# Gate build of a PEER layer: float32 products for every other u block, gate blocks stored by expert

## The chip, the cores and the metric

The kernel runs on one core of a Trainium2 chip. The metric is the device time of one execution in microseconds. Its engines are TensorE (PE, with its weight loads as PEld), VectorE (DVE), ScalarE (ACT) and GpSimd (POOL), and the queue of SyncE (SP) issues most of the DMAs.

## The reference, cut to what matters

The model is two transformer blocks on 512 tokens of width 1024. The change lies in the expert layer (PEER) of the first block, which the reference writes as a gather:

```
q = (xb @ w_query).reshape(128, 8, 2, 128)
s = einsum('chpd,hpnd->chpn', q, sub_keys)
top_s, top_i = lax.top_k(s, 16)             # two lists of 16 of 128 keys
cand_s = top_s[:, :, 0, :, None] + top_s[:, :, 1, None, :]
cand_i = top_i[:, :, 0, :, None] * 128 + top_i[:, :, 1, None, :]
best_s, pos = lax.top_k(cand_s, 16);  idx = take_along_axis(cand_i, pos)
g = softmax(best_s)
act = gelu(einsum('cd,chkd->chk', xb, expert_u[idx]))
out = einsum('chk,chkd->cd', g * act, expert_v[idx])
```

There are 16384 experts, and each token uses 8 x 16 of them.

## The kernel before, in words

The first 128 tokens are done by gathering: GpSimd fetches the rows of u and v that they need, and VectorE multiplies them (L1078, L1084, L1092). The other 384 tokens (TD) are done densely: all 16384 experts are cut into 128 blocks of 128, and for block b the kernel computes acts(b) = gelu(u(b) h) (384 tokens in the free dimension), multiplies by the gates of that block, and adds the product with v(b) into six PSUM banks named vac. A gate is zero where a token does not use an expert.

**Split products.** A float32 weight tile wr that the Stream class has loaded is split by ACT into a high part wh (L110) and by another engine into a low part wl (L111); each product is then three fp32r matmuls (L198 to L200, in lin and mm3). The hidden state hA is split in the same way; hD is its part for the 384 tokens. The stream holds four wr tiles (WR = 4); add names the tiles in the order in which they are loaded, and get splits three tiles ahead. For the u blocks of the gate build the low part is made on GpSimd (lo=G).

**Gate build** (L1027 to L1035). The gates are built from one-hot matrices, eight tokens (GS) at a time, in 48 groups. For each group VectorE makes oj and oi (L995) and og, the second one times the gate (L1002); TensorE multiplies them token by token into a 128 x 128 tile pG (L1018, L1019), and ACT copies it into a stage tile st (L1020). One st holds all 128 blocks of 128 experts for 64 tokens (ST); there are two. When an st is full, SP writes it to DRAM in four DMAs, one for each quarter of the blocks (gates, L1024). Between the groups, u blocks 12 to 33 are multiplied (u_side: pA), so that 34 blocks of acts (AHEAD) are ready before the main loop.

**Main loop** (L1118 on). Step b multiplies u block b + 34, loads the gates of block b + 3 (gate_load: gt, L1049), makes the weighed activations of block b + 1 (weigh, L1053 to L1056), and multiplies block b with v. Beside it run the gathers for the first 128 tokens, whose row tiles lie where st lay.

The order on each engine is made when the kernel is built, by a scheduler that may move instructions within the dependences; each engine then runs its list in order. SP issues its DMAs in list order, waiting where a buffer is still in use.

Of the kernel before, what the change touches and what calls it, by code (L numbers as in the profile page):

```python
# [20 lines left out]
P = 128  # L21
S = 512
D = 1024
# [11 lines left out]
AHEAD = 34  # L35
ST = 64
ROWS, LAG = 7, 5
# [7 lines left out]
FNV = (1, 3)  # L45
GSCALE = 4096.0
WR, WH, SD = 4, 5, 3
RB = 1
# [29 lines left out]
class Stream:  # L78


    def __init__(self, nc, pool):
        self.nc, self.pool, self.items, self.out, self.raw = nc, pool, [], {}, {}
        self.d = self.s = 0

    def add(self, key, src, dest=None, lo=None):
        self.items.append((key, src, dest, lo))
# [9 lines left out]
    def _split(self):  # L96
        i = self.s
        if self.d <= i:
            self._load()
        key, src, dest, lo_eng = self.items[i]  # L100
        n = src.shape[1]
        raw = self.raw.pop(i)
        if dest is None:
            hi = self.pool.tile([P, 512], FR, name=f"wh{i}", tag="wh", bufs=WH)[:, :n]
            lo = self.pool.tile([P, 512], FR, name=f"wl{i}", tag="wl", bufs=WH)[:, :n]
        else:
            hi, lo = dest()
        if len(hi.shape) == 3:
            raw = raw.rearrange("p (k n) -> p k n", n=P)
        self.nc.scalar.activation(hi, raw, AF.Copy)  # L110
        (lo_eng or self.nc.vector).tensor_tensor(lo, raw, hi.bitcast(FT), op=OP.subtract)  # L111
        self.out[key] = (hi, lo)
        self.s += 1
# [43 lines left out]
def body(ctx, tc, a):  # L157
# [253 lines left out]
    n_early = len(u_at) + U_TAIL  # L411

    def add_u(b, **kw):
        for c in range(2):
            ws.add(("u", b, c), a["uT"][b][:, c * 512:(c + 1) * 512], **kw)

    for m in range(16):
        for c in range(2):
            ws.add(("qy", m, c), a["w_query"][m][:, c * 512:(c + 1) * 512], lo=G)
        if m in u_at:  # L420
            add_u(u_at[m], lo=G)
    for b in range(len(u_at), AHEAD):
        add_u(b, lo=G)
    late = {}

# [352 lines left out]
    late["h0"] = h0  # L778
    hn = pk.tile([P, D], FT, name="hn")
    gw0 = pk.tile([P, P], FT, name="gw0")  # L780
    idx = pk.tile([P, P], I32, name="idx")
# [196 lines left out]

    gd = [nc.dram_tensor(f"gates{q}", (TD // ST, P, P // 4, ST), FT, kind="Internal").ap() for q in range(4)]
    ps = ps.then(pA=2, pG=4, rest=2)  # L980
    s1 = ExitStack()
    pg = pool(s1, "pgb", OGB)

    def u_side(b):
        w = [ws.get(("u", b, c)) for c in range(2)]
        pa_ = ps.tile([P, TD], FT, name=f"pA{b}", tag="pA")
        lin(pa_, w, KD, slice(0, TD), lambda k: hD[:, 0, k], lambda k: hD[:, 1, k])
        last["gelu"] = A.activation(acts[:, b % AA], pa_, AF.Gelu).ins  # L988
# [21 lines left out]
    def gate_sum(g, oj, og):  # L1010
# [10 lines left out]
        if t0 + GS == ST:  # L1021
            st = stage.pop(n)
            for q in range(4):
                nc.sync.dma_start(gd[q][n], st[:, q * (P // 4):(q + 1) * (P // 4)])  # L1024

    hot = []
    NG = TD // GS  # L1027
    for i in range(NG):
        hot.append(gate_hot(i))
        if len(hot) > 1:  # L1030
            gate_sum(*hot.pop(0))
        for b in range(n_early + i * (AHEAD - n_early) // NG, n_early + (i + 1) * (AHEAD - n_early) // NG):
            u_side(b)
    while hot:
        gate_sum(*hot.pop(0))  # L1035
    s1.close()

# [4 lines left out]
    act = pac.tile([P, P], FT, name="act")  # L1042
    acc = pac.tile([P, D], FT, name="acc")
    late["tile"] = lambda n, nm: pac.tile([P, n], FR, name=f"late{nm}")
    gates = {}

    def gate_load(b):
        gates[b] = pg.tile([P, TD], FT, name=f"gt{b}", tag="gt", bufs=4)
        nc.sync.dma_start(gates[b].rearrange("p (n t) -> p n t", t=ST), gd[b // 32][:, :, b % 32].rearrange("n j t -> j n t"))  # L1049

# [60 lines left out]
    vac = [ps.tile([P, 512], FT, name=f"vac{i}", tag=f"vac{i}") for i in range(6)]  # L1111
    for b in range(3):
        gate_load(b)
# [461 lines left out]
```

## Time and profile before

| | us |
|---|---|
| median of 3 runs | 2120.83 (2117.81 to 2125.31) |
| profiled execution | 2124.07 |
| its span | 2122.3 |
| TensorE busy | 2033.1 (96%) |
| VectorE busy | 1540.5 (73%) |
| ScalarE busy | 884.8 (42%) |
| GpSimd busy | 645.1 (30%) |
| DMA packets | 267426, of them 119297 under 512 bytes |

The gate build runs from about 462 to 629 us of the span, the main loop from there to about 1540 us. Shares over the whole span hide stages: the same engine can be the bound in one and wait in the next. A row of a stretch gives for each engine its busy time and count, then the granted TensorE clock as a part of full speed, the mean busy share of the 16 DMA engines, and GB/s. "Idle before" in a row is the time for which the engine waited, and the name behind it is what ended the wait.

### The profile page before, as it was taken

How to read it: one execution, taken by the hardware profiler on the slowest of the kernel's cores; microseconds unless marked ns; L12 is line 12 of the kernel's file. 1: busy time of each engine (PE TensorE's matmuls, PEld its weight loads, DVE VectorE, ACT ScalarE, POOL GpSimd, SP SyncE). 2: the span in 40 equal slices, each digit the busy share in tenths (PEclk: the TensorE clock that was granted, in tenths of full speed). 3: DMA queues.
4: the chain of work that ended last, by engine and by line, in shares of the span. 5: the costliest groups of instructions: out<-in, count | busy, mean ns of one | idle time of the engine just before them, and what ended most of it. 6: DMA issues, size and time to landing. Idle time of an engine off the chain costs nothing.

```text
span 2122.3 us, 31628 instructions
## 1 busy us (share of the span) xinstructions
PE 2033.1 (96%) x10907; PEld 1738.9 (82%) x10907; DVE 1540.5 (73%) x3202; ACT 884.8 (42%) x1748; POOL 645.1 (30%) x545
## 2 busy tenths in 40 slices
PE   7999989889998999999999999999989999999999
PEld 5765778788887899999999999988868578888887
DVE  7879879999986877777777777768887854333322
ACT  4477443255553443333433333344443744333321
POOL 2235325765523433333333333323123400000000
PEclk9989999999999999999999999999989999999999
DMA  7514522225669999999998999989943122222332
GB/s 267 179 45 161 182 84 76 90 90 197 251 227 315 353 312 309 301 296 307 295 307 294 312 294 303 301 269 316 300 134 100 41 65 75 96 98 97 97 115 74
DMA packets 267426, 425.90 MB, mean 201 GB/s; under 512 B 119297, under 2 KB 123265, under 8 KB 264194
## 3 DMA queue, kind: packets, MB, share of 16 engines
q1 hardware_dynamic: 224866, 284.15, 40.9%
q0 software_dynamic: 36864, 134.23, 18.5%
q10 hardware_dynamic: 5536, 5.51, 0.9%
q8 instruction: 85, 1.39, 0.3%
q14 instruction: 75, 0.61, 0.1%
HBM read 391.83 MB, written 29.36 MB: 198 GB/s over the span
## 4 chain that ended last, share of the span: by engine, by line
PE 72%; DVE 19%; DMA 3%; issue 2%; ACT 2%; POOL 1%; SPq 0%; ACTq 0%; DVEq 0%; POOLq 0%
PE vac L199 7%; PE vac L200 7%; PE vac L198 7%; PE pA L198 6%; PE pA L199 6%; PE pA L200 6%; DVE og L1002 3%; DVE oi L995 2%; PE pd L199 2%; PE pd L198 2%; PE pd L200 2%; PE upp L200 2%; PE upp L199 2%; PE upp L198 2%; PE gatep L199 2%
## 5 line engine op out<-in xcount | busy, mean ns | idle before, releaser
L110 ACT ACTIVATE wh<-wr 128x512 fp32r<-128x512 f32 x716 | 448.4, 629 | 883.0 <-PE vac L200 220.2
L111 DVE TENSOR_TENSOR wl<-wr,wh 128x512 fp32r<-128x512 f32 x616 | 427.1, 697 | 404.7 <-ACT wh L110 403.4
L198 PE MATMUL pA<-hA,wh 128*128 128x384 f32 x928 | 315.7, 340 | 8.8 <-ACT acts L988 4.7
L200 PE MATMUL pA<-hA,wl 128*128 128x384 f32 x928 | 313.2, 338 | 0.0
L199 PE MATMUL pA<-hA,wh 128*128 128x384 f32 x928 | 312.5, 337 | 0.0
L200 PE MATMUL vac<-wh,wwl 128*128 128x512 f32 x759 | 297.7, 392 | 0.0
L199 PE MATMUL vac<-wl,wwh 128*128 128x512 f32 x759 | 297.4, 392 | 0.0
L198 PE MATMUL vac<-wh,wwh 128*128 128x512 f32 x759 | 296.3, 390 | 0.0
L1078 POOL DMA_INDIRECT ur<-in_u_dram,idx x128 | 157.8, 1233 | 298.0 <-DVE acc L1092 236.0
L1078 POOL DMA_INDIRECT vr<-in_v_dram,idx x128 | 149.0, 1164 | 294.6 <-DVE ur L1084 251.6
L111 POOL TENSOR_TENSOR wl<-wr,wh 128x512 fp32r<-128x512 f32 x100 | 153.4, 1543 | 132.6 <-ACT wh L110 132.4
L198 PEld LDWEIGHTS pA<-hA,wh 128*128 128x128 f32 x928 | 175.6, 189 | 14.7 <-ACT acts L988 6.9
L199 PEld LDWEIGHTS pA<-hA,wh 128*128 128x128 f32 x928 | 175.5, 189 | 3.5
L200 PEld LDWEIGHTS pA<-hA,wl 128*128 128x128 f32 x928 | 175.4, 189 | 0.3 <-DVE wl L111 0.2
L200 PEld LDWEIGHTS vac<-wh,wwl 128*128 128x128 f32 x759 | 142.7, 188 | 29.9
L199 PEld LDWEIGHTS vac<-wl,wwh 128*128 128x128 f32 x759 | 142.8, 188 | 28.0
L198 PEld LDWEIGHTS vac<-wh,wwh 128*128 128x128 f32 x759 | 143.0, 188 | 27.6
L1092 DVE SCALAR_TENSOR_TENSOR acc<-vr,act,acc 128x1024 f32<-128x1024 f32 x127 | 162.7, 1281 | 0.0
L1084 DVE SCALAR_TENSOR_TENSOR ur<-ur,hn 128x1024 f32<-128x1024 f32 x128 | 156.0, 1221 | 0.0
L1055 ACT ACTIVATE wwh<-w 128x384 fp32r<-128x384 f32 x128 | 65.4, 511 | 24.0 <-DVE w L1053 23.7
L1053 DVE TENSOR_TENSOR w<-acts,gt 128x384 f32<-128x384 f32 x128 | 71.0, 555 | 5.6 <-DMA gt<-gates 5.5
L1056 DVE TENSOR_TENSOR wwl<-w,wwh 128x384 fp32r<-128x384 f32 x128 | 70.8, 553 | 4.4 <-ACT wwh L1055 4.1
(677 smaller groups left out, 4010.9 us busy)
## 6 DMA issues: line engine op xcount, KB each, us to landing
wr<-in_uT_dram SPq DMA_DIRECT2D x256, 256.0 KB, 3.9
wr<-in_v_dram SPq DMA_DIRECT2D x256, 256.0 KB, 5.5
wa<-in_w_adaT_dram SPq DMA_DIRECT2D x48, 512.0 KB, 4.3
gates<-st SPq DMA_DIRECT2D x24, 1024.0 KB, 7.5
gt<-gates SPq DMA_DIRECT2D x128, 192.0 KB, 6.0
wr<-in_w_gate_dram SPq DMA_DIRECT2D x44, 256.0 KB, 2.8
wr<-in_w_up_dram SPq DMA_DIRECT2D x44, 256.0 KB, 2.7
wr<-in_w_down_dram SPq DMA_DIRECT2D x44, 256.0 KB, 2.7
```

Of the source, the lines that this page charges most:

```text
L110: self.nc.scalar.activation(hi, raw, AF.Copy)
L111: (lo_eng or self.nc.vector).tensor_tensor(lo, raw, hi.bitcast(FT), op=OP.subtract)
L198: T.matmul(out, lh, rh, start=start, stop=False)
L199: T.matmul(out, lh, rl, start=False, stop=False)
L200: return T.matmul(out, ll, rh, start=False, stop=stop).ins
L1002: V.tensor_tensor(og.rearrange("p (s t) i -> p s t i", t=4), oi.rearrange("p s i t -> p s t i"), gp32[:, tt].rearrange("p (s t) -> p s t", ...
L1053: V.tensor_mul(w, acts[:, b % AA], gates.pop(b))
L1055: A.activation(wh, w, AF.Copy)
L1056: last["w"] = V.tensor_tensor(wl, w, wh.bitcast(FT), op=OP.subtract).ins
L1078: G.indirect_dma_start(out=r, out_offset=None, in_=a[kind], in_offset=bass.IndirectOffsetOnAxis(ap=idx[:, j:j + 1], axis=0))
L1084: V.scalar_tensor_tensor(r, r, 1.0, hn, op0=OP.mult, op1=OP.mult, accum_out=act[:, j:j + 1])
L1092: V.scalar_tensor_tensor(acc, r, act[:, j:j + 1], acc, op0=OP.mult, op1=OP.add)
```

## The change

1. Of the u blocks of the gate build, every other one (12, 14, ... 32) is "whole": its tile is not split, and each product is one float32 matmul with hF, the float32 sum of hD's two parts, which GpSimd makes in two instructions before the build. The whole blocks keep their wr tile until TensorE has read it.
2. The other u blocks of the build (13, 15, ... 33) are still split, but the low part is now made on VectorE.
3. A stage holds 48 tokens (6 groups) where it held 64; there are eight of them. The DRAM tensors of the gates are laid out with all 384 tokens of an expert in a row: a stage is written in rows of 48 values (192 bytes), and a block is read in rows of 384 values (1536 bytes). Before, a stage was written in rows of 32 x 64 values (8 KB) and a block read in rows of 64 values (256 bytes).
4. The gates of blocks 0 and 1 are also copied on ACT into gfirst, which lies in the tile acc (which is first written when the first gathered row of v is used), and are not loaded.
5. u block 33 is multiplied behind the last group, outside the loop.

```diff
-ST = 64
+ST = 48
+GF = 2
     def _split(self):
...
+        if key in self.whole:
+            self.out[key] = raw
+            self.s += 1
+            return
...
+    def whole_u(b):
+        return n_early <= b < AHEAD and (b - n_early) % 2 == 0
...
-    for b in range(len(u_at), AHEAD):
+    for b in range(len(u_at), n_early):
         add_u(b, lo=G)
+    for b in range(n_early, AHEAD):
+        add_u(b, whole=whole_u(b))
...
+    acc = pk.tile([P, D], FT, name="acc")
+    gfirst = acc[:, :GF * TD].rearrange("p (b t) -> p b t", t=TD)
...
-    gd = [nc.dram_tensor(f"gates{q}", (TD // ST, P, P // 4, ST), FT, kind="Internal").ap() for q in range(4)]
+    gd = [nc.dram_tensor(f"gates{q}", (P // 4, P, TD), FT, kind="Internal").ap() for q in range(4)]
...
+    hF = pg.tile([P, KD, TD], FT, name="hF", tag="hF", bufs=1)
+    for k in range(0, KD, 4):
+        G.tensor_tensor(hF[:, k:k + 4], hD[:, 0, k:k + 4].bitcast(FT), hD[:, 1, k:k + 4].bitcast(FT), op=OP.add)
...
-        lin(pa_, w, KD, slice(0, TD), lambda k: hD[:, 0, k], lambda k: hD[:, 1, k])
+        if whole_u(b):
+            for k in range(KD):
+                T.matmul(pa_, w[k // 4][:, k % 4 * P:(k % 4 + 1) * P], hF[:, k], start=k == 0, stop=k == KD - 1)
+        else:
+            lin(pa_, w, KD, slice(0, TD), lambda k: hD[:, 0, k], lambda k: hD[:, 1, k])
...
+            A.activation(gfirst[:, :, n * ST:(n + 1) * ST], st[:, 0:GF], AF.Copy)
             for q in range(4):
-                nc.sync.dma_start(gd[q][n], st[:, q * (P // 4):(q + 1) * (P // 4)])
+                nc.sync.dma_start(gd[q][:, :, n * ST:(n + 1) * ST].rearrange("i j t -> j i t"),
+                                  st[:, q * (P // 4):(q + 1) * (P // 4)])
...
-        for b in range(n_early + i * (AHEAD - n_early) // NG, n_early + (i + 1) * (AHEAD - n_early) // NG):
+        for b in range(n_early + i * (AHEAD - 1 - n_early) // NG, n_early + (i + 1) * (AHEAD - 1 - n_early) // NG):
             u_side(b)
     while hot:
         gate_sum(*hot.pop(0))
+    u_side(AHEAD - 1)
...
-        nc.sync.dma_start(gates[b].rearrange("p (n t) -> p n t", t=ST), gd[b // 32][:, :, b % 32].rearrange("n j t -> j n t"))
+        nc.sync.dma_start(gates[b], gd[b // 32][b % 32])
...
-    for b in range(3):
+    for b in range(GF):
+        gates[b] = gfirst[:, b]
+    for b in range(GF, 3):
         gate_load(b)
```

On SP's list, at the first stage that is written, there stood before (wr is a half of a u block, gates a quarter of the stage):

```order
L92 DMA wr_5609<-in_uT_dram 128x512
L92 DMA wr_5615<-in_uT_dram 128x512
L1024 DMA gates<-st_5284 128x2048 x4
L92 DMA wr_5700<-in_uT_dram 128x512
L92 DMA wr_5706<-in_uT_dram 128x512
L92 DMA wr_5816<-in_uT_dram 128x512
```

and now, up to the second stage:

```order
L96 DMA wr_5397<-in_uT_dram 128x512
L1049 DMA gates<-st_5280 128x32x48
L96 DMA wr_5403<-in_uT_dram 128x512
L1049 DMA gates<-st_5280 128x32x48 x3
L96 DMA wr_5492<-in_uT_dram 128x512
L96 DMA wr_5494<-in_uT_dram 128x512
L96 DMA wr_5585<-in_uT_dram 128x512
L96 DMA wr_5591<-in_uT_dram 128x512
L1049 DMA gates<-st_5512 128x32x48
```

Each write keeps its place between the same loads, and its row at DRAM is 48 values where it was 2048.

On SP's list at the end of the build, from the last stage on, there stood before (gt is a block of gates, wr from in_v_dram a half of a v block):

```order
L1024 DMA gates<-st_7033 128x2048 x4
L92 DMA wr_7460<-in_uT_dram 128x512
L92 DMA wr_7466<-in_v_dram 128x512
L92 DMA wr_7504<-in_v_dram 128x512
L1049 DMA gt_7404<-gates 128x6x64
L1049 DMA gt_7406<-gates 128x6x64
L1049 DMA gt_7408<-gates 128x6x64
```

and now:

```order
L1049 DMA gates<-st_6882 128x32x48
L96 DMA wr_7063<-in_v_dram 128x512
L96 DMA wr_7069<-in_uT_dram 128x512
L1049 DMA gates<-st_6882 128x32x48 x3
L96 DMA wr_7110<-in_uT_dram 128x512
L96 DMA wr_7116<-in_v_dram 128x512
L96 DMA wr_7175<-in_v_dram 128x512
L1075 DMA gt_7161<-gates 128x384
```

The second half of u block 35 (wr_7110) and both halves of v block 1 stand behind the last write; u block 34 and the first half of v block 0 stand ahead of it. The loads of gate blocks 0 and 1 are gone.

On GpSimd's list at the start of the build there stood before:

```order
L111 TENSOR_TENSOR wl_5120<-wr_5047,wh_5119 128x512
L111 TENSOR_TENSOR wl_5180<-wr_5079,wh_5179 128x512
L111 TENSOR_TENSOR wl_5186<-wr_5085,wh_5185 128x512
L111 TENSOR_TENSOR wl_5218<-wr_5117,wh_5217 128x512
L111 TENSOR_TENSOR wl_5224<-wr_5123,wh_5223 128x512
```

and now:

```order
L119 TENSOR_TENSOR wl_5121<-wr_5048,wh_5120 128x512
L119 TENSOR_TENSOR wl_5181<-wr_5080,wh_5180 128x512
L1002 TENSOR_TENSOR hF<-hA 128x1536 x2
L1104 DMA ur_7245<-in_u_dram,idx 128x1024
L1104 DMA ur_7247<-in_u_dram,idx 128x1024
```

After the sum hF, GpSimd has nothing until the gathers of the main loop.

## Rows read from the trace of the kernel before

**Rows 1.** Stretches: length, busy (count) of PE, PEld, DVE, ACT, POOL; clock, DMA, GB/s.
```profile
510.00:530.00 20.00, 18.90 (x176) 18.11 (x174) 19.97 (x18) 11.98 (x23) 11.73 (x6) 1.00 0.44 166
640.00:660.00 20.00, 16.00 (x63) 13.42 (x62) 7.27 (x12) 5.15 (x9) 6.30 (x6) 0.83 1.04 315
660.00:680.00 20.00, 17.26 (x80) 15.65 (x79) 15.98 (x30) 7.26 (x15) 9.19 (x7) 0.91 0.88 277
800.00:900.00 100.00, 100.00 (x508) 91.00 (x507) 74.67 (x114) 38.79 (x72) 33.72 (x28) 1.00 0.91 301
```

**Rows 2.** Groups on DVE and POOL, 461.5 to 632: count, busy, mean ns, idle before.
```profile
L1002 DVE TENSOR_TENSOR og<-oi,gp 128x1024 f32<-128x1024 f16 x48 | 73.6, 1534 | 0.0
L995 DVE TENSOR_TENSOR oi<-iT,ioth 128x1024 f16<-128x1024 f16 x48 | 55.8, 1197 | 0.1
L995 DVE TENSOR_TENSOR oj<-iT,ioth 128x1024 f16<-128x1024 f16 x48 | 40.0, 833 | 0.5 <-PE pG L1019 0.4
...
L111 POOL TENSOR_TENSOR wl<-wr,wh 128x512 fp32r<-128x512 f32 x44 | 79.9, 1819 | 76.0 <-ACT wh L110 76.0
```

**Rows 3.** DVE and POOL in order of time near 531: start, length, instruction.
```profile
531.10 1.21 DVE L1002 TENSOR_TENSOR og<-oi,gp 128x1024 f32<-128x1024 f16 x1
...
532.23 1.85 POOL L111 TENSOR_TENSOR wl<-wr,wh 128x512 fp32r<-128x512 f32 x1 [2.81 <-ACT wh L110]
532.24 0.68 DVE L995 TENSOR_TENSOR oj<-iT,ioth 128x1024 f16<-128x1024 f16 x1
...
532.84 2.31 DVE L1002 TENSOR_TENSOR og<-oi,gp 128x1024 f32<-128x1024 f16 x1
```

**Rows 4.** PE in order of time: u block 32, group 47, u block 33; float32 scores.
```profile
622.95 0.42 PE L198 MATMUL pA<-hA,wh 128*128 128x384 f32 x1
...
627.22 0.25 PE L1018 MATMUL pG<-og,oj 128*128 128x128 f16 x1
...
628.14 0.22 PE L1019 MATMUL pG<-og,oj 128*128 128x128 f16 x1
...
628.35 0.44 PE L198 MATMUL pA<-hA,wh 128*128 128x384 f32 x1
...
159.31 1.98 PE L268 MATMUL mlsc<-km,qm 128*128 128x512 f32 x4
```

**Rows 5.** DMA of four stretches (496:498, 657:660, 643:645, 900:1000): packets; queue share of 16 engines.
```profile
DMA packets 121, 0.86 MB, mean 430 GB/s; under 512 B 16, under 2 KB 16, under 8 KB 16
...
DMA packets 1803, 0.83 MB, mean 275 GB/s; under 512 B 1598, under 2 KB 1598, under 8 KB 1803
q1 hardware_dynamic: 1791, 0.80, 112.5%
...
DMA packets 1257, 0.66 MB, mean 328 GB/s; under 512 B 1064, under 2 KB 1064, under 8 KB 1257
q1 hardware_dynamic: 1257, 0.66, 112.2%
...
DMA packets 20623, 30.29 MB, mean 303 GB/s; under 512 B 10749, under 2 KB 10749, under 8 KB 20617
...
q1 hardware_dynamic: 16433, 14.99, 46.7%
```

**Rows 6.** DMA issues (470:490, then 496:498): count, KB each, us to landing.
```profile
wr<-in_uT_dram SPq DMA_DIRECT2D x6, 256.0 KB, 2.8
...
wr<-in_uT_dram SPq DMA_DIRECT2D x1, 256.0 KB, 10.3
```

**Rows 7.** First and last stage copy; last writes, PE and POOL at the loop's start.
```profile
L1020 ACT ACTIVATE st<-pG x96: 577/598/627, 471.1 to 628.7; 128x512 f32<-128x512 f32 x96
...
629.30 4.55 SPq L1024 DMA_DIRECT2D gates<-st  x4
...
645.44 0.69 PE L198 MATMUL pA<-hA,wh 128*128 128x384 f32 x1 [4.00 <-ACT wh L110]
...
643.20 0.94 POOL L1078 DMA_INDIRECT ur<-in_u_dram,idx  x1 [23.99 <-DMA gates<-st]
```

More of the change, by code (lines that the diff above doesn't have):

```diff
@@ L82, in __init__, with add @@
         self.nc, self.pool, self.items, self.out, self.raw = nc, pool, [], {}, {}
+        self.whole = set()
         self.d = self.s = 0
-    def add(self, key, src, dest=None, lo=None):
+    def add(self, key, src, dest=None, lo=None, whole=False):
+        if whole:
+            self.whole.add(key)
         self.items.append((key, src, dest, lo))
@@ L1042, in body @@
     act = pac.tile([P, P], FT, name="act")
-    acc = pac.tile([P, D], FT, name="acc")
     late["tile"] = lambda n, nm: pac.tile([P, n], FR, name=f"late{nm}")
```

## The prediction

> **What bounds the kernel now.** I read the table by stretch first, for the gate build and the main loop. The reader should see that the two have different bounds. In the main loop TensorE is busy for all 100.00 of 100 us at full clock [rows 1]; DMA at a share of 0.91 costs nothing there. So the lighter gate reads, the DMA time that they free and the idle engines beside them can give nothing in that stage: a gain or a loss must come from the build and from the step into the loop. In the build (510 to 530) VectorE is busy 19.97 of 20 us and TensorE 18.90, DMA 0.44 [rows 1]: VectorE sets the pace. Second, the groups of VectorE in the build and their neighbours in time: an og that runs beside nothing takes 1.21 us, and one beside a low part on GpSimd 2.31 [rows 3]. The 144 one-hot instructions were busy 73.6 + 55.8 + 40.0 = 169.4 us [rows 2], less 144 x 0.08 by which neighbours overlap, 158 us. Undisturbed ones start 0.60 (oj or oi) and 1.14 us (og) behind each other, from 531.10, 532.24 and 532.84 [rows 3]: 48 x (0.60 + 0.60 + 1.14) = 112 us. The other 46 us are what 44 low parts on GpSimd cost VectorE, some 1.05 us each. Third, the step into the loop: TensorE waits 4.00 us until 645.44 for a split half of a u block [rows 7], and 640 to 680 has 4.0 + 2.7 us idle and clocks of 0.83 and 0.91 [rows 1].
>
> **The change part by part.**
>
> VectorE. The 44 low parts leave GpSimd, and 20 to 22 of them come to VectorE. A low part there has no row in the build; the nearest is the undisturbed oj, 0.68 us [rows 3], so 22 x 0.7 = 15 us. hF is 2 x 1536 columns, six times a low part, on GpSimd at the start: at some 1.1 us of disturbance each, 7 us. VectorE then needs 112 + 15 + 7 = 134 us for the build, less than TensorE (below), which is next.
>
> TensorE. A split u block takes 627.22 - 622.95 = 4.27 us (24 matmuls), a group of eight tokens 628.14 - 627.22 + 0.06 = 0.98 us, both when nothing is waited for [rows 4]. For the whole block there is the float32 product of the scores: one 128x512 product shows as two records, and four records take 1.98 us, of which the last one's tail belongs to nobody else, so 0.43 to 0.50 us a record, 0.86 to 0.99 a product [rows 4]; for 384 columns 0.65 to 0.74, and eight of them 5.2 to 5.9, taken as 5.5 us. Whole blocks cost TensorE 1.2 us more each, 13 us for eleven: this part alone is a loss. From the first group to the last (blocks 12 to 32 lie between) TensorE has 48 x 0.98 + 10 x 4.27 + 11 x 5.5 = 47 + 43 + 60 = 150 us. In the trace the first stage copy starts at 471.1 and the last at 628.7 [rows 7], 157.6 us. If TensorE alone set the pace, the build would end some 8 us earlier, at 621.
>
> ACT loses 22 high parts and gets eight small copies for gfirst; it is busy 11.98 of 20 us [rows 1], so both lie beside TensorE's work.
>
> The writes. Eight stages of 4 x 4096 rows are 131072 pieces of 192 bytes, where 8 KB rows went out before. The trace has no small write. Its nearest rows are the reads of the gates, in pieces of 256 bytes. Large pieces move at 430 GB/s [rows 5], 26.9 GB/s an engine, so a 2 KB piece is 76 ns. From 657 to 660 one queue is served, and all 16 engines work: 48 us of engine time for 1598 small pieces and 193 of 2 KB, (48 - 14.7) / 1598 = 20.8 ns each. From 643 to 645: (32 - 14.7) / 1064 = 16.3 ns. In the main loop, beside the gathers' queue: (747 - 5684 x 0.076) / 10749 = 29 ns [rows 5]. I take 20.8, from the longest stretch in which this queue has the engines for itself, and keep 16.3 and 29 as ends. Then the writes take 131072 x 20.8 / 16 = 170 us of all engines, in a build of 150. By bytes alone (192 at 26.9 GB/s, 7 ns) it would be 58 us; above, a write could cost more than the read, and nothing in the trace excludes it.
>
> Who waits for them. The loads of the u blocks stand on the same queue, in the order of SP's list. That they stand behind a write also in time is shown by the load that landed 10.3 us after its issue, beside 2.8 without a write ahead [rows 6]. There are two stage tiles, so a stage can be filled only when the write two before is done; ACT waits for that with its copies, behind them the gelus and high parts on its list, and TensorE with the next group. So a build whose writes need longer than TensorE runs at the pace of the writes.
>
> The sum. The first write can go when six groups and two blocks are done: 471 + 6 x 0.98 + 4.3 + 5.5 = 487. From there to the last write's end the queue has 131072 pieces and the 39 halves of u and v that SP's list puts between: 170 + 39 x 0.61 (128 pieces of 76 ns over 16 engines) = 170 + 24, ends at 681. The half of u block 35 that TensorE needs next stands right behind; with its load, high and low part some 2.5 us, 683.5. In the trace the same wait ends at 645.44 [rows 7]: +38. Of that comes back: v block 0 and half of block 35 are already done by then (18 matmuls at the loop's 100 / 508 = 0.2 us [rows 1], 3.6 us), and of the 2.7 us idle and the 5 us of lost clock behind it (0.17 and 0.09 of 20 us) [rows 1] some 2, since TensorE comes out of a longer pause and the gathers start at the same moment: GpSimd waits for the last write here too, 23.99 us before [rows 7]. The missing loads of gate blocks 0 and 1 and the reads in rows of 1536 bytes are within this. In all +38 - 6 = +32 or 33 us. Per ns of a piece's price it is 8.2 us more or less; at 16.8 ns the change is worth nothing.
>
> The profiled execution took 2124.07 us (span 2122.3), the median is 2120.83, 3.2 less. So 2124.1 + 32.7 = 2156.8 for an execution like the profiled one, 2153.5 for the median.
>
> **The rivals.**
>
> The writes keep up. Below some 16 ns a piece the queue is ready before TensorE, and the build is TensorE's: it ends at 621, the last write at about 637, the wait at 639, so -6, and -6 more from the step into the loop: -12, or 2109. At 16.3 it is -4. [...]
>
> [...]
>
> In between, at 16 to 17.6 ns a piece, gains and waits cancel, within 0.3%: 2121.
>
> The change does not free VectorE, since only GpSimd's operations of a certain kind disturb it: rows 3 show the very instruction that leaves, so I give this nothing of its own.
>
> **How the numbers follow.** Two runs of this kernel can be told apart by about 0.3%, 6.4 us. The forecast, writes as the bound at 17.6 to 29 ns, +7 to +100, gets 0.52; writes that keep up or nearly so, -6 to -14, 0.24; in between 0.10; dear writes, above +100, 0.14. The likeliest is the forecast: 2153.5. The range takes the first three, from -15 to +101: 2106 to 2222; it leaves out the dear writes and little else. Faster 0.24, same 0.10, slower 0.66.
>
> **What would show it.** og should take 1.2 us with nearly none above 2, and VectorE have idle time in the build. The stage copies on ACT should wait for DMAs of gates, the DMA share be near 1 from 490 to 680, and TensorE have 25 us and more without work there. Eleven blocks should show 16 records each, some 5.5 us together. In the main loop TensorE should be as before, 100 of 100 us. The prediction is wrong if the last write ends less than 20 us behind the last group with no copy waiting for one (writes cheap), or if the build lasts past 730 (dear).

## The result and the profile after

The changed kernel takes 2158.29 us (median of four runs, 2155.90 to 2160.11) where the kernel before takes 2122.60 beside it: 1.017 times as long, 95% interval 1.0147 to 1.0193. It is slower by some 36 us. The profiled execution took 2159.39 us (span 2157.6), 35.3 more than the one of before.

The main loop is what it was. These are the stretches of the changed kernel, with the columns of [rows 1]:

```profile
510.00:530.00 20.00, 20.00 (x160) 16.18 (x158) 17.86 (x24) 8.11 (x16) 0.00 (x0) 1.00 1.42 158
550.00:570.00 20.00, 12.14 (x67) 9.06 (x66) 9.84 (x14) 5.30 (x10) 0.00 (x0) 0.74 1.15 208
610.00:630.00 20.00, 10.75 (x96) 9.15 (x96) 13.42 (x17) 3.83 (x9) 0.00 (x0) 0.83 1.47 162
650.00:670.00 20.00, 10.71 (x37) 9.52 (x36) 3.84 (x6) 4.50 (x8) 5.88 (x6) 0.66 1.18 304
670.00:690.00 20.00, 10.90 (x43) 9.59 (x44) 5.09 (x10) 4.09 (x8) 0.00 (x0) 0.78 0.99 247
800.00:900.00 100.00, 100.00 (x507) 91.01 (x506) 75.64 (x119) 39.11 (x75) 34.25 (x30) 1.00 0.89 300
```

800 to 900 reads as in [rows 1], TensorE 100.00 of 100 us. The build does not: in three of four stretches from 550 to 690 TensorE has work for a little over half of the time, and its granted clock falls with it, to 0.66. VectorE no longer sets the pace either (13.42 of 20 us at 610). What everybody waits for is in the view of the stage tile st, first the copies into it on ScalarE (line 1044), the writes out of it (1049) and the copies of the two kept blocks (1047): count, shortest/median/longest ns, first and last start; then the idle time ahead of them and who waited for them.

```profile
L1044 ACT ACTIVATE st<-pG x96: 581/598/629, 466.3 to 648.0; 128x512 f32<-128x512 f32 x96
L1049 SPq DMA_DIRECT2D gates<-st x32: 378/3926/11372, 485.4 to 673.7; - x32
L1047 ACT ACTIVATE acc<-st x8: 282/282/286, 485.4 to 648.7; 128x96 f32<-128x96 f32 x8
...
  DMA gates<-st: 34.9, 4
...
  PE pG L1042: 22.2, 4
```

The copies into st stood four times, 34.9 us in all, for the write that had to leave the same tile first; TensorE stood 22.2 us for those copies. The last copy starts at 648.0, where it was 628.7 [rows 7], though the first starts 4.8 us sooner (466.3, 471.1): from first to last copy the build takes 181.7 us where it took 157.6. In order of time on ScalarE, with the idle time and its releaser in brackets, the four waits are those ahead of stages 3, 4, 6 and 7:

```profile
533.77 2.06 ACT L1044 ACTIVATE st<-pG 128x512 f32<-128x512 f32 x4 [7.51 <-DMA gates<-st]
...
558.69 2.06 ACT L1044 ACTIVATE st<-pG 128x512 f32<-128x512 f32 x4 [10.80 <-DMA gates<-st]
...
603.54 2.06 ACT L1044 ACTIVATE st<-pG 128x512 f32<-128x512 f32 x4 [3.86 <-DMA gates<-st]
...
629.89 2.06 ACT L1044 ACTIVATE st<-pG 128x512 f32<-128x512 f32 x4 [12.69 <-DMA gates<-st]
...
684.88 0.63 ACT L118 ACTIVATE wh<-wr 128x512 fp32r<-128x512 f32 x1 [13.62 <-DMA wr<-in_uT_dram]
```

The last of these rows is the step into the loop: the half of u block 35 stood 13.62 us for its load, and TensorE then 8.78 us for that half:

```profile
685.57 0.69 PE L206 MATMUL pA<-hA,wh 128*128 128x384 f32 x1 [8.78 <-ACT wh L118]
```

SyncE's queue says why, the last writes and the weight load behind them:

```profile
661.56 15.98 SPq L1049 DMA_DIRECT2D gates<-st  x3
677.64 4.09 SPq L96 DMA_DIRECT2D wr<-in_uT_dram  x1
```

So the time went where small writes are the bound of the build (24.1 us more from first to last copy), and then a second time behind the last stage, whose writes nothing hides: 35.3 - 24.1 + 4.8 = 16 us.

What was meant to be freed was freed. The groups on VectorE from 461.5 to 690, as in [rows 2]:

```profile
L1026 DVE TENSOR_TENSOR og<-oi,gp 128x1024 f32<-128x1024 f16 x48 | 58.4, 1217 | 0.0
L1019 DVE TENSOR_TENSOR oi<-iT,ioth 128x1024 f16<-128x1024 f16 x48 | 34.7, 752 | 0.2
L1019 DVE TENSOR_TENSOR oj<-iT,ioth 128x1024 f16<-128x1024 f16 x47 | 32.3, 687 | 23.9 <-PE pG L1043 23.8
L119 DVE TENSOR_TENSOR wl<-wr,wh 128x512 fp32r<-128x512 f32 x29 | 19.5, 689 | 66.0 <-ACT wh L118 65.9
```

og takes 1217 ns where it took 1534 on average [rows 2], and VectorE has 90 us of idle time in this stretch, which runs on into the step to the loop. It is time that the build could not use.

### The profile page after: what moved, and what is told of

It reads as the page before. It is cut to its first block, busy times and chain, and to the rows that moved or that the text cites. A ratio compares the mean times of both kernels' runs of the same rounds, so it can differ in the third digit from the quotient of the medians.

```text
span 2157.6 us, 31389 instructions
## 1 busy us (share of the span) xinstructions
PE 2049.7 (95%) x10819; PEld 1729.8 (80%) x10819; DVE 1510.7 (70%) x3224; ACT 874.3 (41%) x1734; POOL 567.4 (26%) x503
## 4 chain that ended last, share of the span: by engine, by line
PE 75%; DVE 12%; DMA 5%; ACT 2%; SPq 2%; issue 2%; POOL 1%; ACTq 0%; DVEq 0%; POOLq 0%
PE vac L207 8%; PE vac L208 8%; PE vac L206 7%; PE pA L206 6%; PE pA L208 6%; PE pA L207 6%; SPq L1049 2%; PE pd L206 2%; PE pd L207 2%; PE pd L208 2%; PE upp L208 2%; PE upp L207 2%; DMA gates<-st 2%; PE upp L206 2%; PE gatep L207 2%
## 5 line engine op out<-in xcount | busy, mean ns | idle before, releaser
L118 ACT ACTIVATE wh<-wr 128x512 fp32r<-128x512 f32 x694 | 434.2, 629 | 850.9 <-PE vac L208 260.9
L119 DVE TENSOR_TENSOR wl<-wr,wh 128x512 fp32r<-128x512 f32 x638 | 440.5, 694 | 457.7 <-ACT wh L118 456.0
L206 PE MATMUL pA<-hA,wh 128*128 128x384 f32 x840 | 286.2, 341 | 18.8 <-ACT wh L118 17.2
L208 PE MATMUL pA<-hA,wl 128*128 128x384 f32 x840 | 284.6, 339 | 1.1 <-DVE wl L119 1.1
L207 PE MATMUL pA<-hA,wh 128*128 128x384 f32 x840 | 283.6, 338 | 0.0
L1104 POOL DMA_INDIRECT ur<-in_u_dram,idx x128 | 148.3, 1159 | 486.6 <-DVE acc L1118 244.8
L1104 POOL DMA_INDIRECT vr<-in_v_dram,idx x128 | 152.3, 1189 | 299.7 <-DVE ur L1110 259.1
L206 PEld LDWEIGHTS pA<-hA,wh 128*128 128x128 f32 x840 | 159.5, 190 | 25.2 <-ACT wh L118 18.0
L207 PEld LDWEIGHTS pA<-hA,wh 128*128 128x128 f32 x840 | 159.5, 190 | 3.4
L208 PEld LDWEIGHTS pA<-hA,wl 128*128 128x128 f32 x840 | 159.3, 190 | 2.3 <-DVE wl L119 2.3
L119 POOL TENSOR_TENSOR wl<-wr,wh 128x512 fp32r<-128x512 f32 x56 | 73.2, 1322 | 55.6 <-ACT wh L118 55.2
L1012 ACT ACTIVATE acts<-pA 128x384 f32<-128x384 f32 x116 | 55.2, 476 | 54.5 <-PE pA L1009 30.0
L1042 PE MATMUL pG<-og,oj 128*128 128x128 f16 x384 | 51.3, 226 | 25.9 <-ACT st L1044 22.2
```

What stands on the lines that cost most here:

```text
L206: T.matmul(out, lh, rh, start=start, stop=False)
L207: T.matmul(out, lh, rl, start=False, stop=False)
L208: return T.matmul(out, ll, rh, start=False, stop=stop).ins
L1042: T.matmul(pt[:, t], oj[:, h, :, t], o[:, :, 1], start=True, stop=False)
L1104: G.indirect_dma_start(out=r, out_offset=None, in_=a[kind], in_offset=bass.IndirectOffsetOnAxis(ap=idx[:, j:j + 1], axis=0))
```

## Experiments

The theory: the 131072 writes of 192 bytes bound the build and the step into the loop; the rest of the change is worth little either way. Rivals: the whole float32 blocks cost TensorE the time; or it is not the rate of the writes but their place in SyncE's one queue, ahead of the weight loads. Where a run is compared with another, the copies into st are the surest sign, because they begin and end the build. Its length, from the first copy to the last, says more than the time of the last: the first copy lies between 463.2 and 473.6 in the profiled executions, and that goes with TensorE's granted clock from 100 to 150 us, far ahead of the change (0.97 with 466.3 in the changed kernel, 0.86 with 471.1 before).

**The old layout in DRAM, all else changed.** The write and the read are those of before, with stages of 48.

```
-    gd[q]: (P // 4, P, TD)
+    gd[q]: (TD // ST, P, P // 4, ST)
-    write gd[q][:, :, n * ST:(n + 1) * ST].rearrange("i j t -> j i t")
+    write gd[q][n]
-    read gd[b // 32][b % 32]
+    read gd[b // 32][:, :, b % 32].rearrange("n j t -> j n t")   # 8 pieces a row
```

> The changed kernel with one part undone: the gates lie in DRAM by stage again (a stage is written in rows of 32 x 48 values, 6 KB; a block is read in eight pieces of 192 bytes). Whole blocks, low parts on VectorE, stages of 48 and the two blocks kept on chip stay. If the small writes are the loss: the build is TensorE's, the last stage copy comes at about 620 where it came at 648.0, no stage copy waits for a write, time 2105 to 2112. If the float32 blocks or the place of the loads are the loss: the build stays near 648, time above 2140.

Measured: 2118.86 us, 0.9957 of before (0.9941 to 0.9972). From the tile st and the stretches of this run:

```profile
L1044 ACT ACTIVATE st<-pG x96: 581/600/624, 471.8 to 624.1; 128x512 f32<-128x512 f32 x96
```

```profile
510.00:530.00 20.00, 20.00 (x172) 16.85 (x171) 16.06 (x22) 11.25 (x23) 0.00 (x0) 1.00 0.66 239
550.00:570.00 20.00, 20.00 (x156) 16.17 (x155) 16.58 (x22) 9.30 (x20) 0.00 (x0) 1.00 0.60 218
```

No copy waits for a write, and 40 us of the changed kernel's time are gone with this one edit: the layout was the loss. The gain that stays over before (2126.91 us beside these runs) is 8 us; the time lies above the expected 2105 to 2112. The build shows why: TensorE is busy for 20.00 of 20 us, and from the first copy to the last it takes 624.1 - 471.8 = 152.3 us. The rest of the change had traded a bound by VectorE (157.6 us) for one by TensorE that is nearly as long.

**No whole blocks.** The changed kernel with every u block split.

```
-        return n_early <= b < AHEAD and (b - n_early) % 2 == 0
+        return False
```

> The changed kernel without whole blocks: all u blocks of the build are split, low parts on VectorE. The writes by expert stay. If the writes are the bound: no change, 2153 to 2162, with stage copies waiting for writes as before, since TensorE's 11 x 0.9 us and VectorE's 22 x 0.7 us lie beside them. If the float32 blocks are the loss: 10 us less or more, 2148 or below.

Measured: 2158.52 us, 1.0137 (1.0102 to 1.0173), the changed kernel's time again. Its copies into st run to 648.2 and wait as they did:

```profile
L1044 ACT ACTIVATE st<-pG x96: 578/598/627, 471.4 to 648.2; 128x512 f32<-128x512 f32 x96
...
  DMA gates<-st: 31.9, 5
```

TensorE's arithmetic is off the path that sets the end here; the first rival is out.

**Each piece in a slot of 256 bytes.** The writes of the changed kernel go at two rates. Packets and rate of its DMA, first from 592 to 596, then from 608 to 619:

```profile
DMA packets 3915, 0.75 MB, mean 187 GB/s; under 512 B 3915, under 2 KB 3915, under 8 KB 3915
...
DMA packets 8310, 1.59 MB, mean 145 GB/s; under 512 B 8310, under 2 KB 8310, under 8 KB 8310
```

16 engines x 4 us / 3915 = 16.3 ns a piece; 16 x 11 / 8310 = 21.2 ns. Stages 0, 3, 4 and 7 have the first rate (186 to 190 GB/s from 500 to 503, 570 to 572, 592 to 596 and 677 to 681), 1, 2, 5 and 6 the second (144 to 146 from 520 to 524, 539 to 545, 608 to 619 and 643.5 to 645). A piece of stage n starts 192 n bytes into its row of 1536, and in just these four it runs over a multiple of 256. The waits above fit: stages 3, 4 and 7 stood 7.51, 10.80 and 12.69 us for the writes of 1, 2 and 5, stage 6 only 3.86 for those of 4, and stage 5 not at all for those of 3. The edit gives each piece a slot of 256 bytes of its own, as many pieces and as many bytes written; the reads become eight pieces.

```
-    gd[q]: (P // 4, P, TD)
+    gd[q]: (P // 4, P, TD // ST, 64)
-    write gd[q][:, :, n * ST:(n + 1) * ST]
+    write gd[q][:, :, n, :ST]
```

> The changed kernel with each row of 48 values (192 bytes) in a slot of its own of 256 bytes, so that no row crosses a multiple of 256 bytes; as many pieces and bytes are written as before, a block is read in eight pieces. In the changed kernel stages 0, 3, 4 and 7 are written at 187 GB/s (16.4 ns a piece) and stages 1, 2, 5 and 6, whose rows cross a multiple of 256 bytes, at 145 (21.2 ns). If the crossing is the cause: all eight stages at 187, 4 x 4.9 = 20 us less writing, time 2134 to 2143. If something else makes the slow stages (loads beside them, the order of the quarters): some stages still at 145, time 2152 to 2164.

Measured: 2148.65 us, 1.0091 (1.0058 to 1.0124). The first line is the DMA from 538 to 546, in stage 2, one of the slow ones; the others are from the tile st:

```profile
DMA packets 7556, 1.46 MB, mean 183 GB/s; under 512 B 7555, under 2 KB 7555, under 8 KB 7555
```

```profile
L1044 ACT ACTIVATE st<-pG x96: 578/598/634, 469.2 to 637.6; 128x512 f32<-128x512 f32 x96
...
  DMA gates<-st: 20.5, 4
```

This stage now runs near the fast rate (16 x 8 / 7556 = 16.9 ns a piece), and so does stage 5 (some 185 GB/s from 607 to 612): the boundary was the price. In the changed kernel pieces of stages 3 and 7 don't start on a boundary either and are fast, since they run over none. The 21.2 - 16.3 = 4.9 ns between the rates is what running over a boundary costs a piece here; by what mechanism, no run shows. From first to last copy the build takes 168.4 us where the changed kernel took 181.7, and the time is 10 us less. I had expected 15 to 24: the cheaper half saves 65536 x 4.9 / 16 = 20 us of DMA time, and I had taken nearly all of it for time on the path. The waits of the copies fell by 14.4 us and the build by 13.3; the last copy is only 10.4 us earlier because this execution began its build 2.9 us later.

**The low parts on VectorE, nothing else.** The kernel before with the low parts of u blocks 12 to 33 taken from GpSimd.

```
     for b in range(len(u_at), n_early):
         add_u(b, lo=G)
+    for b in range(n_early, AHEAD):
+        add_u(b)
```

> The kernel before with one edit: the low parts of the u blocks of the build are made on VectorE (44 of them), not on GpSimd. If GpSimd's subtractions stretch VectorE's one-hot instructions by some 1.05 us each: VectorE needs 112 + 44 x 0.68 = 142 us for the build, TensorE 137, the build shrinks from 157.6 to 143 to 147 us, time 2106 to 2112. If VectorE's long instructions have another cause: VectorE gets 30 us more work, time 2140 to 2152.

Measured: 2104.60 us, 0.9893 (0.9853 to 0.9933): faster than before, and the lowest median of all that was run. VectorE's groups from 461.5 to 610, one stretch, and the copies into st:

```profile
L1004 DVE TENSOR_TENSOR og<-oi,gp 128x1024 f32<-128x1024 f16 x47 | 57.3, 1219 | 0.0
L111 DVE TENSOR_TENSOR wl<-wr,wh 128x512 fp32r<-128x512 f32 x48 | 32.7, 688 | 7.7 <-ACT wh L110 5.3 <-PE pG L1021 2.2
L997 DVE TENSOR_TENSOR oj<-iT,ioth 128x1024 f16<-128x1024 f16 x47 | 32.2, 685 | 0.0
L997 DVE TENSOR_TENSOR oi<-iT,ioth 128x1024 f16<-128x1024 f16 x47 | 31.2, 685 | 0.0
```

```profile
510.00:530.00 20.00, 20.00 (x195) 19.53 (x193) 19.86 (x29) 12.29 (x26) 0.00 (x0) 1.00 0.79 295
```

```profile
L1022 ACT ACTIVATE st<-pG x96: 584/602/625, 466.0 to 605.7; 128x512 f32<-128x512 f32 x96
```

VectorE takes 44 instructions of 0.69 us more and is done sooner, since the one-hot instructions are short again (og at 1.22 us). VectorE and TensorE are now both full (19.86 and 20.00 of 20), and the build takes 139.7 us. Beside the 152.3 us of the run with whole blocks this prices them: from first to last copy TensorE is busy for 150.18 us there and 139.70 here, 10.5 us more for eleven, 0.95 each. Another 2.1 us there are idle time, which makes 12.6, and the two times differ by 14 us. The two kernels differ in the length of a stage and in the kept blocks too, which these rows don't separate. So the good part of the change is the one that empties GpSimd; multiplying whole takes it back.

**Without the two kept blocks.** The changed kernel loads gate blocks 0 and 1 like the others.

```
-            A.activation(gfirst[:, :, n * ST:(n + 1) * ST], st[:, 0:GF], AF.Copy)
-    for b in range(GF):
-        gates[b] = gfirst[:, b]
-    for b in range(GF, 3):
+    for b in range(3):
         gate_load(b)
```

> The changed kernel without its two kept gate blocks: the eight copies into gfirst are gone and gate blocks 0 and 1 are loaded from DRAM like the others. If the kept blocks are worth what the sum gave them (part of the 6 us back: two loads of 128 rows and their wait, behind the last write), the time is 2161 to 2166 us beside 2158.3. Rival: VectorE multiplies the second kept block only at 686.15 us, after the wait for u block 35 (wh at 684.88), and a load issued at 682 lands by then, so the kept blocks are worth nothing: 2157 to 2160 us.

Measured: 2164.36 us, 1.0184 (1.0161 to 1.0207), in the range expected if the kept blocks are worth something. But the interval overlaps that of the changed kernel (1.0147 to 1.0193), and in the profiled execution the first copy into st is already 7.3 us later (473.6), ahead of all that the kept blocks touch, and with it the last (657.3). In the 60 us behind the last copy TensorE is busy for 39.95 us here and for 41.61 in the changed kernel. So what they are worth at the loop's start is small, and whether it is anything stays open.

**Gates by expert where the pieces are 256 bytes.** The kernel with the low parts on VectorE, stages of 64 as before, and the changed kernel's layout: 98304 pieces of 256 bytes, each on its boundary. Then the same with the first two blocks kept in two free places of acts.

```
-    gd[q]: (TD // ST, P, P // 4, ST)
+    gd[q]: (P // 4, P, TD)
     write and read as in the changed kernel
```

> The kernel before with the low parts of u blocks 12 to 33 on VectorE (2104.6 us), and with its gates in DRAM by expert in stages of 64 positions: pieces of 256 B that start on multiples of 256 B, 98304 of them, and each gate block read back in one piece. Theory (the writes cost only where the stream of them is longer than the build): at the 187 GB/s of the stages that crossed no boundary a stage of 4.19 MB takes 22.4 us, under the 23.3 us that a stage of the 140 us build lasts, so the last copy into st stays at 605 to 608 us; the last stage lands 8 us later than its 14 us before, and the gathers, which waited for it until 620.26 us, start at about 628; the time is 2106 to 2115 us. Rival A: reads in one piece give more than the late start costs, 2096 to 2103 us. Rival B: SyncE stands behind each stage's writes (16 to 18 us in the changed kernel), the weight loads behind them come late, and the build gets longer: last copy after 615 us, 2118 to 2135 us.

> The same with the first two gate blocks also copied on chip, into the two free places of acts, and not loaded: six copies of 128 x 2 x 64 on ScalarE more, two loads fewer. If the loads of the first blocks wait behind the last stage's writes and someone waits for them, it is 3 to 6 us faster than the run without the copies; if nobody waits for them (rival), within 2 us of it.

Measured: 2137.73 us, 1.0060 (1.0040 to 1.0079), and 2137.05, 1.0051 (1.0032 to 1.0069). My theory missed by 23 us: I had taken the writes for hidden as long as a stage's 22 us fit into a stage of the build. Its copies into st and SyncE's issues of the writes, then its DMA from 523 to 531:

```profile
L1022 ACT ACTIVATE st<-pG x96: 579/598/624, 467.5 to 629.4; 128x512 f32<-128x512 f32 x96
L1026 SPq DMA_DIRECT2D gates<-st x24: 377/4208/7099, 488.1 to 643.8; - x24
```

```profile
DMA packets 7008, 1.80 MB, mean 225 GB/s; under 512 B 7007, under 2 KB 7007, under 8 KB 7007
```

A piece costs 16 x 8 / 7007 = 18.3 ns, so a stage takes 18.7 us, less than I had assumed, and no copy into st waits for a write. Still the build takes 161.9 us instead of 139.7. It is what rival B of the expectation had said, some 3 us beyond its range: SyncE is held 4.2 us (median) by each of the 24 writes, where it was 0.64 for those of 8 KB rows in the run with the low parts on VectorE, and the weight loads stand behind. The kept blocks change nothing that can be told (second run).

**The same writes from another queue.** The run before (without kept blocks), its writes issued by GpSimd.

```
-                nc.sync.dma_start(gd[q][:, :, n * ST:(n + 1) * ST].rearrange("i j t -> j i t"),
+                G.dma_start(gd[q][:, :, n * ST:(n + 1) * ST].rearrange("i j t -> j i t"),
```

> The kernel of e6_by_expert_64 (2137.7 us, last copy into st at 629.4 us) with one change: the gate writes are issued by GpSimd on its own DMA queue instead of by SyncE, which stood 10 us behind each stage's writes with the weight loads after it. Theory (in e6 the weight loads came late because they stood behind the writes in SyncE's one queue, and with them the u blocks): SyncE's loads go out at once, the last copy into st is back near 606 to 612 us and the time is 2106 to 2118 us. Rival: the 16 DMA engines that both queues share are what the loads wait for, or GpSimd takes long to write out 16384 pieces a stage: the last copy stays after 620 us and the time is 2128 us or more.

Measured: 2112.72 us, 0.9931 (0.9908 to 0.9954).

```profile
L1022 ACT ACTIVATE st<-pG x96: 577/599/636, 463.2 to 606.5; 128x512 f32<-128x512 f32 x96
...
  DMA gates<-st: 2.9, 2
```

The same pieces, 25 us less: in the run before it was their place in SyncE's queue, ahead of the weight loads, that cost the time, and not their number. Nor did they get cheaper. GpSimd's queue moves them in packets of some 3.9 KB, and its row of DMA from 465 to 605 gives their price; the row below it is a wait of TensorE from 465 to 650:

```profile
q0 software_dynamic: 5365, 20.70, 63.7%
...
PE vac L198 <- ACT wwh L1058: 14.6, 1, 14.6
```

16 x 140 x 0.637 = 1427 us for 20.70 MB, 80900 pieces of 256 bytes: 17.6 ns each, where SyncE's queue had 18.3. What stays (8 us over the run with the low parts on VectorE) lies for the most part at the loop's start: the build is only 3.6 us longer (143.3), but behind the last write TensorE stands 14.6 us for the first weighed activations, and VectorE ahead of them 11.9 us for a gate load (3.3 there). The gathers begin later too (635.62 us, 620.26 there); what that alone costs isn't shown.

**Kept blocks in the fastest kernel.**

```
+    gfirst = acts[:, AHEAD:AA]
+            A.activation(gfirst[:, :, n * ST:(n + 1) * ST], st[:, 0:2], AF.Copy)
-    for b in range(3):
+    for b in range(2):
+        gates[b] = gfirst[:, b]
+    for b in range(2, 3):
```

> The kernel of e4_low_on_vector (2104.6 us) with its first two gate blocks copied on chip as well, into the two free places of acts, and not loaded; gates in DRAM by stage as in the kernel before. SyncE took 9.72 us for the first five gate loads at 614.98 us, with weight loads for the first u blocks of the loop behind them. Theory: with two of five gone those weight loads go out 3 to 4 us earlier, 2100 to 2103 us. Rival: the row gathers or the loads themselves hold the start of the loop, so nothing arrives, within 1.5 us of 2104.6 us.

Measured: 2107.28 us, 0.9912 (0.9890 to 0.9934), as much as without them. SyncE's queue at the loop's start, with six gate loads in a row:

```profile
613.02 11.87 SPq L1053 DMA_DIRECT2D gt<-gates  x6
627.43 0.77 SPq L92 DMA_DIRECT2D wr<-in_v_dram  x1
```

Two blocks need no load, and the loads of later blocks move up into the free places, ahead of weight loads as before.

**The changed kernel, writes from GpSimd's queue.** The edit of e8_writes_by_gpsimd, in the changed kernel.

> The changed kernel (2158.3 us) with its gate writes issued by GpSimd on its own queue instead of by SyncE; nothing else. Theory (here the rate of the writes is the bound: the copies into st wait 34.9 us for them in the changed kernel, which they never did in e6_by_expert_64, and 16384 pieces took some 24 us on GpSimd's queue in e8_writes_by_gpsimd, longer than the 17.5 us that ScalarE needs for a stage of 48): the copies into st still wait 20 to 50 us for gate writes, the last one stays after 635 us and the time is 2138 to 2165 us. Rival: also here it was the weight loads standing behind the writes in SyncE's queue; then the last copy comes at 610 to 622 us and the time is 2112 to 2128 us.

Measured: 2167.10 us, 1.0199 (1.0177 to 1.0221). The time is 2 us over the theory's range, and its mechanism fell: no copy waits for a write any more, yet the last one is at 666.2. SyncE's waits from 465 to 650 name somebody else; the fourth row is ScalarE's, from 465 to 700:

```profile
SPq L96 <- PE pA L1009: 61.9, 20, 5.1
SPq L96 <- DVE wl L119: 60.5, 20, 12.1
SPq L96 <- DMA wr<-in_uT_dram: 55.5, 17, 7.5
...
ACT wh L118 <- DMA wr<-in_uT_dram: 99.3, 18, 12.8
```

Twenty times the next weight load waited until TensorE had read a whole block (line 1009) out of its landing places. A split block frees them as soon as its high and low parts are made; a whole one holds them through its eight products. With loads that land late this starves TensorE (from 465 to 600 VectorE waits 38.1 us for high parts and TensorE 21.7 for og); with the old layout SyncE waits for line 1009 as well (16 times, 38.8 us), and there TensorE stays busy. The last run takes the whole blocks out of this kernel.

> The kernel of e10_after_writes_by_gpsimd (2167.1 us, last copy into st at 666.2 us) with every u block split, none multiplied whole. In e10 ScalarE waited 99.3 us for loads of weights, which a whole block holds in their landing places until TensorE has read them. Theory A (the whole blocks' hold on the landing places delays the loads): the last copy comes at 612 to 630 us, the time is 2115 to 2132 us. Theory B (131072 pieces, half of them over a 256 B boundary, fill the DMA engines so that the loads are late in any case): the last copy stays after 645 us and the time is 2145 to 2168 us.

Measured: 2137.06 us, 1.0052 (1.0033 to 1.0071); the copies into st:

```profile
L1044 ACT ACTIVATE st<-pG x96: 579/601/707, 465.8 to 635.1; 128x512 f32<-128x512 f32 x96
...
  DMA gates<-st: 16.0, 4
```

30 us come back, and time and last copy lie between the two theories (A: 2115 to 2132, B: 2145 to 2168). The build is 30.9 us shorter (169.3 for 200.2). Up to some 10 of them can be the price of the whole products themselves; that the other 20 are the hold on the landing places is argued from the waits above, and no run moves the hold alone. What is left is again the writes, which copies wait 16.0 us for: 131072 pieces hold this build up from either queue.

All profiled executions in one table, by span: granted clock from 100 to 150 us, first and last copy into st, the build between them, span (us). The span follows the build in the main; where it doesn't, as in the last two rows, the start of the build and the step into the loop make the difference.

| kernel | clock | first copy | last copy | build | span |
|---|---|---|---|---|---|
| low parts on VectorE | 0.94 | 466.0 | 605.7 | 139.7 | 2103.9 |
| the same, kept blocks | 0.94 | 465.4 | 605.1 | 139.7 | 2106.7 |
| by expert, pieces of 256 B, GpSimd's queue | 0.97 | 463.2 | 606.5 | 143.3 | 2110.9 |
| old layout, stages of 48 | 0.85 | 471.8 | 624.1 | 152.3 | 2119.7 |
| before | 0.86 | 471.1 | 628.7 | 157.6 | 2122.3 |
| by expert, pieces of 256 B, SyncE's queue | 0.93 | 467.5 | 629.4 | 161.9 | 2131.7 |
| the same, kept blocks | 0.97 | 463.6 | 625.4 | 161.8 | 2135.5 |
| changed, no whole blocks, GpSimd's queue | 0.97 | 465.8 | 635.1 | 169.3 | 2135.8 |
| slots of 256 B | 0.90 | 469.2 | 637.6 | 168.4 | 2148.1 |
| changed | 0.97 | 466.3 | 648.0 | 181.7 | 2157.6 |
| changed, no whole blocks | 0.84 | 471.4 | 648.2 | 176.8 | 2158.2 |
| changed, GpSimd's queue | 0.97 | 466.0 | 666.2 | 200.2 | 2170.1 |
| changed, no kept blocks | 0.86 | 473.6 | 657.3 | 183.7 | 2170.2 |

## Why the prediction was right, step by step

It gave 2153.5 us and slower; 2158.3 was measured, within the range, by the mechanism that it had put first. Its own signs are all there: og at 1.22 us, VectorE idle, copies on ScalarE waiting for gates, TensorE without work for over 25 us (22.2 for the copies and 8.78 at the last wait alone), the main loop at 100.00.

The first write was put at 487, and is at 485.4. The wait for u block 35 was to end at 683.5; its high part starts at 684.88 and TensorE goes on at 685.57. That is 40.1 after [rows 7] instead of 38, and of it 40.1 - 35.3 = 4.8 comes back instead of 6. So the terms that make the sum are each within a few us. Times from the span's start hide one more thing: this execution came to its first copy 4.8 us sooner than that of before, at a clock that was higher ahead of the build and that the change has no part in (runs of the changed kernel's family have 0.84 to 0.97 there). Counted from the first copy, the first write comes after 19.1 us and not 16, and TensorE goes on 45.0 us later than before and not 40.1.

Two of them met for a reason that the prediction didn't have. **The price of a piece** was 20.8 ns, from reads of 256 bytes in [rows 5]. It is two prices, 16.3 and 21.2, mean 18.8, so the writes need 131072 x 18.8 / 16 = 154 us and not 170. That they still ended near 681 (the small packets stop at some 682.7) shows in the DMA from 485.4 to 681, packets and the share of SyncE's and of GpSimd's queue:

```profile
DMA packets 136555, 38.93 MB, mean 199 GB/s; under 512 B 130654, under 2 KB 130654, under 8 KB 136542
...
q1 hardware_dynamic: 135534, 35.08, 115.5%
q0 software_dynamic: 1008, 3.67, 5.2%
```

Nearly all small writes lie in it. The weight loads are some 40 of 0.61 us, 24 us as predicted. New is GpSimd's queue: one gather of the loop starts at 648.28 and the others from 658.41 on, beside the last stage's writes, where the prediction had them wait for the last write. Their 3.67 MB take 8.5 us at 430 GB/s. 154 + 24 + 8.5 = 187 of the 197 us up to 682.7; I have not accounted for all of the other 10, some of it are moments in which the queue has nothing, such as 1.5 us near 588. A price too high by a tenth, terms left out and an early start met, so the forecast's point was lucky. Its range was not: both prices lie in the 16.3 to 29 that the reads had given. **The point of no change**, 16.8 ns, was too high: the run with slots has 16 x 8 / 7556 = 16.9 ns and still loses 0.9%. The forecast took a queue that is served faster than TensorE works as free; the runs show that it also delays what stands behind it (by expert, pieces of 256 bytes: 18.7 us a stage where the build had 139.7 / 6 = 23.3 for one, and yet a build 22 us longer).

**TensorE** was right in both terms. A whole block shows as 16 records:

```profile
641.67 5.38 PE L1009 MATMUL pA<-hF,wr 128*128 128x384 f32 x16
```

5.38 us with its last record's tail, predicted 5.5; from its start to the next instruction on TensorE it is 5.21 (641.67 to 646.88), 0.94 more than the 4.27 of a split block [rows 4]. The build by TensorE alone was worked out as 150 us, and is 152.3 in the run with the old layout; the eleven whole blocks were to cost 13 us, and cost 10.5, or 12.6 with the idle time in that run. That run also shows what the rival in which the writes keep up would have brought: its last copy is 4.6 us earlier than in [rows 7], and the time 8 us less, where the prediction had 12.

**VectorE.** 134 us were predicted, 112 + 15 + 7. Its groups from 461.5 on sum to 58.4 + 34.7 + 32.3 = 125 us and 20 low parts of 0.69 to 139, less 163 x 0.08 of overlap 126. The 7 us for hF were right in size but not in place: its two sums run on GpSimd from 455.57 for 7.67 us, and the first oj and oi beside them, at 455.88 and 459.79, take 3.98 and 3.99 us instead of 0.68. These 6.6 us lie ahead of the first copy into st, and most of them ahead of the stretch that was summed. That a subtraction on GpSimd costs VectorE some 1.05 us, worked out from [rows 3], is confirmed by the run that only moves these: og falls from 1534 ns to 1219 and, in the same view, oi from 1197 to 685 and oj from 833 to 685, so 48 x 0.975 us for 44 instructions, 1.06 each. The build is 157.6 - 139.7 = 18 us shorter, and no more, because the 44 low parts take some 44 x 0.6 = 26 us of VectorE's time there (two in a row take 1.29 us at 621.60 in the kernel before), so that some 20 of the 47 are left, and because TensorE is next.

**The rivals.** Writes that keep up, below some 16 ns a piece: measured 16.3 where nothing crosses a boundary and 21.2 where a piece does. Dear writes, above +100: no run shows the price that this takes; pieces of 192 bytes cost 16.3 and 21.2 ns, within what the reads of 256 had shown (16.3 to 29). The kept blocks, which the sum had within its 6 us, show no effect clear of the scatter in any of three kernels.

What stays open: the 10 us above, and by which single waits the build of e6_by_expert_64 got longer. That SyncE's queue was the cause is shown by moving the writes, and its row shows it held; the waits of TensorE that are listed there, 8.1 us for low parts and 7.0 for og, are only 15 of some 22 us.

## What to carry to other kernels

A layout that makes reads whole makes the writes small: count the pieces and price them, since here 131072 pieces of 192 bytes, 25 MB, take the DMA time of 66 MB in large ones (154 us at the 430 GB/s of [rows 5]), and look at what stands behind them on the same queue, for it can pay first: 22 us of build here with pieces of 256 bytes, where no copy waited for a write. When one edit frees an engine, ask what it takes on in exchange and which engine is next: VectorE's 46 us of disturbance were worth 18, because the work that caused them went to VectorE itself and TensorE needs 140 of the 158, and an edit that lengthens TensorE's work by 10 to 13 took most of that. Try the parts of a change alone: here one was worth 1.1%, and the others together lost 2.8% (1.0170 / 0.9893).

## What the runs showed of the hardware that I had not expected

- A write of 192 bytes costs 16.3 ns of a DMA engine where it lies within one block of 256 bytes, and 21.2 ns where it runs over a boundary; one of 256 bytes on its boundary costs 18.3 ns. Small reads of the same matrix had shown 16.3 to 29.
- The same 98304 writes made a build of 139.7 us 22 us longer from the queue that also carries its weight loads (467.5 to 629.4), and 4 us from another queue (463.2 to 606.5), though the DMA view counts both queues against the same 16 engines (63.7% and 22.0% from 465 to 605) and a piece costs nearly as much there (17.6 ns, 18.3 on SyncE's queue). SyncE is held 4.2 us (median) by an issue of 4096 such pieces, 0.64 by one of as many bytes in rows of 8 KB.
- Two sums on GpSimd of 7.67 us together stretched the two VectorE instructions beside them from 0.68 to 3.98 and 3.99 us.
- GpSimd, when it issues such writes, is held 1.69 us (median of 24) for each of the four issues of a stage; it has nothing else to do in that time.
- TensorE's granted clock fell to 0.66 in stretches where it stood for half of the time, and was back at 1.00 in the main loop.
